# One encoder layer with attention and a recurrent branch: the elementwise work around the merge of its branches, written for VectorE in place of GpSimd

## The chip, the cores and the metric

The kernel runs on one core of a Trainium2 chip. The metric is the device time of one execution in microseconds. A core has five instruction queues that each run in program order: TensorE (PE, with its weight loads shown as PEld), VectorE (DVE), ScalarE (ACT), GpSimd (POOL) and SyncE (SP, which here issues DMAs). They wait for each other through semaphores.

## What is computed

Two request groups, 1024 and 256 tokens, share all weights and run as 1280 columns. Cut to what matters here:

```
h = rmsnorm(x, norm_mix) * (1 + sc1) + sh1;  p = h @ w_in
o_mla  = mla_branch(p_mla) @ w_mla_o
y      = wkv_scan(forward) + wkv_scan(backward)
mu, var = mean and variance of y over each head of 64
yn     = (y - mu) * rsqrt(var + LNX_EPS) * lnx_w + lnx_b
out    = (yn + bonus) * g;      o_rwkv = out @ w_rwkv_o
x = x + g1 * ((sigmoid(gate_m) * o_mla + sigmoid(gate_r) * o_rwkv) @ w_out)
h = rmsnorm(x, norm_ffn) * (1 + sc2) + sh2      (the second norm)
x = x + g2 * ((silu(u) * z) @ w_ffn_out);  u, z = split(h @ w_ffn_in)
return rmsnorm(x, final_norm)
```

## The kernel before, in words

Activations lie with channels on the 128 partitions (eight tiles of 128 channels) and tokens along the free axis. A product of f32 accuracy is made of three passes in the rounded format fp32r: each operand is split into a high part (a cast on ACT) and a low part (the f32 value minus the high part), and PE sums high x high, low x high and high x low. A weight tile comes by DMA into `wraw`, ACT makes `whi` (L53), and a subtraction makes `wlo` (L55). `split_w` takes the engine of that subtraction as an argument and uses POOL if none is given. Activations are split by `split_in` (L1023 on ACT, then L1024, on DVE if no engine is given).

The order of instructions on each engine is made by a scheduler from the program's order and priorities; each engine then runs its list in order. The stage around the change goes like this.

- While the recurrent scan ends (its last triangular inversion is the alternating pair L865 and L867 on DVE), PE fills in the gate products and the attention output product (`mla_out`, with its sums L1172 and the low parts of its weights on POOL). The first `branch` call, for the columns 256 to 768, runs beside it.
- `branch` loads the two scan outputs `y` and `yb`, adds them (L1064), subtracts the mean of each head (L1065 to L1067), squares on ACT (L1068), sums (L1069), makes the inverse deviation in a few small operations (L1071 to L1076), scales (L1078), transposes on PE (L1085), multiplies (L1086), adds the bonus (L1087) and splits the result (`or`, L1023 and L1024). It is called three times; the second and third calls, for the late columns, are spread through the first merge.
- `merge` runs first for the early columns (256 to 768) and then for the late ones (768 to 1280 and 0 to 256). For each of eight output tiles `dt` it has a product with `w_rwkv_o` (L1041, four weight tiles deep, one `split_w`), a multiplication by the gate (L1102), the addition of the attention part `xm` (L1103) and a split into `h2h` and `h2l` (L1023, L1024). Then, again for eight tiles, comes the product with `w_out` (two `split_w`) and the residual (L1115). `gt` and `xm` come by DMA into a pool of four row buffers, so that two `dt` are in flight in the early merge and one, of two pieces each, in the late merge. The split weights have two buffers.
- `norm2` squares and sums x1 (L1212 on ACT, L1213), multiplies by the inverse norm (L1217) and by the modulation (L1221), and splits (L1023, L1024), two tiles of three on POOL. It runs for the early columns inside the late merge, and for the late ones inside the first FFN product.
- The FFN after it (`gemm`, L67) is one unbroken row of matmuls.

The buffer counts of the row, product and weight pools stand in one line:

```
QB, MR, FR, KS, FP, RB, WB = 3, 4, 4, 4, 2, 2, 2
```

Of the kernel before, what the change touches and what calls it, by code (L numbers as in the profile page):

```python
# [18 lines left out]
KT = D // P  # L19
# [1006 lines left out]

def weights(g, src, kt):
    return [split_w(g, src[:, k0:k0 + 4, :], 4, pool=g.fl, tag=g.ft, rbufs=RB, bufs=WB) for k0 in range(0, kt, 4)]


def product(g, src, kt, parts, ws=None):

    ws = ws or weights(g, src, kt)
    for part in parts:
# [12 lines left out]
def branch(g, c0, n, tile_, row, out, ps):  # L1047
# [12 lines left out]
    for w in range(nw):  # L1060
        y, yb = tile_("y"), row("yb")
        for t, nm in ((y, "y0"), (yb, "y1")):
            nc.sync.dma_start(out=t, in_=g.scr[nm][c0 + w * P:c0 + (w + 1) * P, :])
        nc.gpsimd.tensor_tensor(y, y, yb, ALU.add)  # L1064
        nc.vector.tensor_reduce(mean[:, 8 * w:8 * w + 8], heads(y), AX.X, ALU.add)  # L1065
# [11 lines left out]
    for w, y in enumerate(ys):  # L1077
        (nc.gpsimd if w % 2 else nc.vector).tensor_tensor(heads(y), heads(y), each(rs, w), ALU.mult)  # L1078
    for j in range(4):
# [6 lines left out]
        nc.vector.tensor_tensor(wg, wg, p, ALU.mult)  # L1086
        nc.gpsimd.tensor_tensor(wg, wg, bg, ALU.add)  # L1087
        split_in(g, wg, out[0][:, j, :], out[1][:, j, :])


def merge(g, spans, ops, m, x1, row):
# [3 lines left out]
    for dt in range(KT):  # L1095
        ts = []
        for c, (c0, n) in zip(cs, spans):
            ts.append((row("gt")[:, :n], row("xm")[:, :n]))
            for t, nm, k in zip(ts[-1], ("gate", "xm"), (8, 0)):
                nc.sync.dma_start(out=t, in_=g.scr[nm][k + dt, :, c])  # L1100
        for p, c, (t, xm) in zip(product(g, io["w_rwkv_o"][dt], 4, [[x] for x in ops]), cs, ts):
            nc.vector.scalar_tensor_tensor(t, t, 1.0, p, ALU.add, ALU.mult)  # L1102
            nc.gpsimd.tensor_tensor(t, t, xm, ALU.add)  # L1103
            split_in(g, t, m[0][:, dt, c], m[1][:, dt, c])
    for dt in range(KT):
        xs = [row("xt")[:, :n] for _, n in spans]
        for c, x in zip(cs, xs):
            nc.sync.dma_start(out=x, in_=io["xT"][dt, :, c])
        for p, x, (c0, n) in zip(product(g, io["w_out"][dt], KT, [[([y[:, :, c] for y in m], n)] for c, (_, n) in zip(cs, spans)]),
                                 xs, spans):  # L1110
            for s, (s0, l) in enumerate(SEG):
# [85 lines left out]
def phase_ffn(g, out, mid):  # L1197
# [8 lines left out]
    def norm2(ms, c0, n):  # L1206
# [8 lines left out]
        for k in range(KT):  # L1215
            h = ms.tile([P, n], F32, tag="q", name="h", bufs=QB)
            nc.vector.tensor_tensor(h, x1[:, k, c], acc, ALU.mult)  # L1217
            for s, (s0, l) in enumerate(SEG):
                lo, hi = max(c0, s0) - c0, min(c0 + n, s0 + l) - c0
                if lo < hi:  # L1220
                    nc.vector.tensor_scalar(h[:, lo:hi], h[:, lo:hi], g.A2[:, k, s:s + 1], g.modT[:, 24 + k, s:s + 1],  # L1221
                                            ALU.mult, ALU.add)
            split_in(g, h, hh[:, k, c], hl[:, k, c], nc.vector if k % 3 == 1 else nc.gpsimd)

# [237 lines left out]
```

## Time and profile before

| | us |
|---|---|
| three runs, median (lowest to highest) | 2691.51 (2689.03 to 2695.47) |
| the profiled execution, its own time | 2687.72 |
| span of its trace | 2686.0 |
| PE busy in the span | 2501.3 (93%) |
| DVE busy | 1426.3 (53%) |
| ACT busy | 998.8 (37%) |
| POOL busy | 800.6 (30%) |
| mean granted clock of TensorE, share of full | 0.958 |

The busy figures are averages over stages with different limits. The stage that the change touches runs from about 1376 to 1780 us after the start of the span. "Idle before" in a row is the time for which the engine stood still just ahead of such an instruction; the name behind an arrow is what ended that time.

### The profile page before, as it was taken

To read this page: it belongs to the slowest core of one execution; us is meant where nothing else is said; L and a number is where in the kernel's file an instruction comes from. 1 tells how busy PE (TensorE), PEld (TensorE's weight loads), DVE (VectorE), ACT (ScalarE), POOL (GpSimd) and SP (SyncE) were. 2 spreads that over 40 slices of the span, in tenths; PEclk is the share of its full clock that TensorE was granted. 3 is DMA by queue.
4 is the path that set the end of the run, shared out by engine and by line. 5 is a ranking of instruction groups with operands and counts; after the bars stand their busy time and mean duration, and the time that the engine had idled before them with its cause. 6 is when DMAs were issued, how large, how long until landed. Compare 5 with 4: busy or idle time off the path is not lost.

```text
span 2686.0 us, 42442 instructions
## 1 busy us (share of the span) xinstructions
PE 2501.3 (93%) x17018; PEld 2121.5 (79%) x17018; DVE 1426.3 (53%) x2399; ACT 998.8 (37%) x1867; POOL 800.6 (30%) x789
## 2 busy tenths in 40 slices
PE   5999999989998799999898898899999999999997
PEld 3777777778887688888886677778888888888886
DVE  5655652357777688886785666552222232222328
ACT  4422332347676765555652233331110111101114
POOL 2112131021015655443434665442111111111123
PEclk7999999999999798899998999999999999999998
DMA  7654532100003545644656754221111111111113
GB/s 285 230 197 174 212 126 84 47 31 19 18 13 89 186 146 173 176 129 139 202 172 193 240 167 144 80 71 56 40 33 39 40 40 40 35 37 40 40 42 132
DMA packets 188470, 292.37 MB, mean 109 GB/s; under 512 B 16160, under 2 KB 106096, under 8 KB 188272
## 3 DMA queue, kind: packets, MB, share of 16 engines
q1 hardware_dynamic: 174880, 242.07, 28.4%
q0 software_dynamic: 5760, 26.22, 2.4%
q10 hardware_dynamic: 7632, 21.37, 2.3%
q8 instruction: 134, 2.20, 0.3%
q14 instruction: 64, 0.52, 0.1%
HBM read 211.95 MB, written 77.64 MB: 108 GB/s over the span
## 4 chain that ended last, share of the span: by engine, by line
PE 72%; DVE 16%; DMA 4%; issue 3%; POOL 2%; ACT 2%; SPq 0%; POOLq 0%; DVEq 0%; ACTq 0%
PE mm L67 43%; PE fp L1041 8%; PE s L627 3%; DVE xt L865 3%; DVE W L867 2%; PE o L661 2%; PE proj L560 2%; PE gps L453 2%; PE t L648 2%; PE pA L820 1%; PE py L913 1%; PE py L931 1%; PE ada_ps L170 1%; PE lora L369 1%; PE pS L925 1%
## 5 line engine op out<-in xcount | busy, mean ns | idle before, releaser
L55 POOL TENSOR_TENSOR wlo<-wraw,whi 128x1024 fp32r<-128x1024 f32 (+3 forms) x197 | 359.5, 1827 | 1168.0 <-ACT whi L53 1151.9
L53 ACT CAST whi<-wraw 128x1024 fp32r<-128x1024 f32 (+2 forms) x212 | 172.7, 818 | 917.3 <-issue 460.4
L67 PE MATMUL mm<-h2h,whi 128*128 128x512 f32 (+1 forms) x1056 | 279.5, 358 | 2.8 <-ACT whi L53 2.7
L67 PE MATMUL mm<-h2h,wlo 128*128 128x512 f32 (+1 forms) x1056 | 278.8, 358 | 2.7 <-POOL wlo L55 2.7
L67 PE MATMUL mm<-h2l,whi 128*128 128x512 f32 (+1 forms) x1056 | 278.3, 357 | 0.0
L67 PE MATMUL mm<-g,whi 128*128 128x512 f32 (+1 forms) x1056 | 240.7, 359 | 6.2 <-DVE ft L1251 5.6
L1041 PE MATMUL fp<-x,whi 128*128 128x256 f32 (+1 forms) x912 | 203.0, 316 | 15.0 <-ACT x L1023 8.3
L67 PEld LDWEIGHTS mm<-g,whi 128*128 128x128 f32 x1056 | 177.8, 190 | 38.0 <-issue 5.7
L67 PEld LDWEIGHTS mm<-h2h,whi 128*128 128x128 f32 x1056 | 177.2, 189 | 34.5 <-ACT whi L53 3.3
L67 PEld LDWEIGHTS mm<-h2h,wlo 128*128 128x128 f32 x1056 | 177.0, 189 | 34.3 <-POOL wlo L55 3.6
L67 PEld LDWEIGHTS mm<-h2l,whi 128*128 128x128 f32 x1056 | 177.1, 189 | 31.3 <-issue 0.5
L1263 DVE SCALAR_TENSOR_TENSOR x<-mm,g2h,x 128x512 f32<-128x512 f32 (+1 forms) x144 | 87.0, 656 | 196.3 <-PE mm L67 196.0
L1041 PEld LDWEIGHTS fp<-x,whi 128*128 128x128 f32 x912 | 153.5, 200 | 25.4 <-ACT x L1023 10.0
L1251 DVE SCALAR_TENSOR_TENSOR ft<-ft,mm 128x512 f32<-128x512 f32 (+1 forms) x66 | 36.0, 593 | 226.9 <-ACT ft L1250 226.9
L67 PE MATMUL mm<-hh,whi 128*128 128x512 f32 (+1 forms) x480 | 148.8, 368 | 6.9 <-ACT pp L320 3.9
L1041 PE MATMUL fp<-x,wlo 128*128 128x256 f32 (+1 forms) x456 | 144.4, 317 | 11.6 <-POOL wlo L55 7.6
L67 PE MATMUL mm<-hl,whi 128*128 128x512 f32 (+1 forms) x480 | 148.2, 365 | 7.0 <-DVE hl L265 6.9
L1252 DVE TENSOR_TENSOR ft<-ft,mm 128x512 f32<-128x512 f32 (+1 forms) x66 | 36.0, 593 | 217.5 <-PE mm L67 217.5
L67 PE MATMUL mm<-hh,wlo 128*128 128x512 f32 (+1 forms) x480 | 146.5, 365 | 0.0
L67 PE MATMUL mm<-g,wlo 128*128 128x512 f32 (+1 forms) x528 | 136.2, 359 | 1.2 <-POOL wlo L55 1.2
L865 DVE TENSOR_TENSOR xt<-W,X 128x126 f32<-128x126 f32 (+22 forms) x310 | 127.6, 412 | 9.0
L867 DVE TENSOR_TENSOR W<-W,xt 128x126 f32<-128x126 f32 (+22 forms) x310 | 125.0, 403 | 8.6
(320 smaller groups left out, 5210.7 us busy)
## 6 DMA issues: line engine op xcount, KB each, us to landing
wraw<-in_w_ffn_in_dram SPq DMA_DIRECT2D x56, 512.0 KB, 3.5
araw<-in_w_ada_dram ACTq DMA_DIRECT2D x32, 512.0 KB, 3.3
wraw<-in_w_ffn_out_dram SPq DMA_DIRECT2D x26, 512.0 KB, 3.6
wraw<-in_w_in_dram SPq DMA_DIRECT2D x20, 512.0 KB, 3.8
x<-scr_h SPq DMA_DIRECT2D x20, 512.0 KB, 7.7
whi<-scr_gw SPq DMA_DIRECT2D x36, 256.0 KB, 3.2
wlo<-scr_gw SPq DMA_DIRECT2D x36, 256.0 KB, 3.5
araw<-in_w_ada_dram SPq DMA_DIRECT2D x16, 512.0 KB, 9.4
```

Source lines behind the costliest of these rows:

```text
L53: nc.scalar.copy(hi, raw)
L55: (eng or nc.gpsimd).tensor_tensor(lo, raw, hi, ALU.subtract)
L67: nc.tensor.matmul(p[:, :n], lhsT=ww[:, k, :], rhs=aa[:, k, c0:c0 + n], start=(k == 0 and i == 0), stop=(k == kt - 1 and i == 2))
L453: nc.tensor.matmul(p[:, :n], lhsT=ww[:, k % 4, :], rhs=aa[:, k, c0:c0 + n], start=(k == 0 and i == 0), stop=(k == KT - 1 and i == 2))
L560: nc.tensor.matmul(p[:, :n], lhsT=ww[:, k, :], rhs=aa[:, k, c0:c0 + n], start=(k == 0 and i == 0), stop=(k == kt - 1 and i == 2))
L627: nc.tensor.matmul(s[:, o:o + w], lhsT=a[:, tt * P:(tt + 1) * P], rhs=b[:, c0 + o:c0 + o + w], start=(m == 0), stop=(m == 2))
L648: nc.tensor.transpose(t[:, j, :], prs[i][:, kk * P:(kk + 1) * P], g.ident)
L661: nc.tensor.matmul(o, lhsT=vs[h // 4][:, c0 // P + kk, h % 4, :], rhs=pts[j][m][kk // 4][:, kk % 4, :], start=(kk == 0 and m == 0), stop=( ...
L865: nc.vector.tensor_tensor(tv, W[:, h:, j:j + 1].broadcast_to([P, n, j]), X[:, j:j + 1, 0:j].broadcast_to([P, n, j]), ALU.mult)
L867: nc.vector.tensor_tensor(W[:, h:, 0:j], W[:, h:, 0:j], tv, ALU.add)
L1041: g.nc.tensor.matmul(p[:, c:c + n], lhsT=ww[:, k % 4, :], rhs=aa[:, k, :n], start=(k == 0 and i == 0), stop=(k == kt - 1 and i == 2))
L1263: nc.vector.scalar_tensor_tensor(x1[:, dt, c0:c0 + n], p[:, :n], g.g2h[:, dt, c0 // TP:c0 // TP + 1], x1[:, dt, c0:c0 + n], ALU.mult, ALU.add)
```

## The change

Every tensor operation that POOL had in `branch`, `merge` and `norm2` is written for DVE: the sums L1064, L1087 and L1103, the scaling L1078 (every second one was on POOL), the low parts of the weights of both merge products (L55, through a new argument of `weights` and `product`) and the low parts of the second norm (L1024, two of three were on POOL). POOL keeps the low parts of the other weights and L1172.

```diff
-def weights(g, src, kt):
-    return [split_w(g, src[:, k0:k0 + 4, :], 4, pool=g.fl, tag=g.ft, rbufs=RB, bufs=WB) for k0 in range(0, kt, 4)]
+def weights(g, src, kt, eng=None):
+    return [split_w(g, src[:, k0:k0 + 4, :], 4, eng, pool=g.fl, tag=g.ft, rbufs=RB, bufs=WB) for k0 in range(0, kt, 4)]
...
-def product(g, src, kt, parts, ws=None):
+def product(g, src, kt, parts, ws=None, eng=None):
...
-    ws = ws or weights(g, src, kt)
+    ws = ws or weights(g, src, kt, eng)
...
-        nc.gpsimd.tensor_tensor(y, y, yb, ALU.add)
+        nc.vector.tensor_tensor(y, y, yb, ALU.add)
...
-        (nc.gpsimd if w % 2 else nc.vector).tensor_tensor(heads(y), heads(y), each(rs, w), ALU.mult)
+        nc.vector.tensor_tensor(heads(y), heads(y), each(rs, w), ALU.mult)
...
-        nc.gpsimd.tensor_tensor(wg, wg, bg, ALU.add)
+        nc.vector.tensor_tensor(wg, wg, bg, ALU.add)
...
-        for p, c, (t, xm) in zip(product(g, io["w_rwkv_o"][dt], 4, [[x] for x in ops]), cs, ts):
+        for p, c, (t, xm) in zip(product(g, io["w_rwkv_o"][dt], 4, [[x] for x in ops], eng=nc.vector), cs, ts):
...
-            nc.gpsimd.tensor_tensor(t, t, xm, ALU.add)
+            nc.vector.tensor_tensor(t, t, xm, ALU.add)
...
-        for p, x, (c0, n) in zip(product(g, io["w_out"][dt], KT, [[([y[:, :, c] for y in m], n)] for c, (_, n) in zip(cs, spans)]),
-                                 xs, spans):
+        for p, x, (c0, n) in zip(product(g, io["w_out"][dt], KT, [[([y[:, :, c] for y in m], n)] for c, (_, n) in zip(cs, spans)],
+                                         eng=nc.vector), xs, spans):
...
-            split_in(g, h, hh[:, k, c], hl[:, k, c], nc.vector if k % 3 == 1 else nc.gpsimd)
+            split_in(g, h, hh[:, k, c], hl[:, k, c], nc.vector)
```

The scheduler makes new lists from it. DVE in the early merge, among the products with `w_rwkv_o`, before (names as above; `gn` holds the small statistics of `branch`):

```order
L1024 TENSOR_TENSOR h2l<-gt,h2h 128x512
L1102 SCALAR_TENSOR_TENSOR gt<-gt,fp 128x512 x2
L1086 TENSOR_TENSOR wg<-wg,yT 128x512 x2
L1024 TENSOR_TENSOR h2l<-gt,h2h 128x512
L1102 SCALAR_TENSOR_TENSOR gt<-gt,fp 128x512
L1024 TENSOR_TENSOR h2l<-gt,h2h 128x512
L1024 TENSOR_TENSOR or<-wg,or 128x512
L1102 SCALAR_TENSOR_TENSOR gt<-gt,fp 128x512
```

and with the change, at the same place:

```order
L55 TENSOR_TENSOR wlo<-wraw,whi 128x512
L1103 TENSOR_TENSOR gt<-gt,xm 128x512
L1102 SCALAR_TENSOR_TENSOR gt<-gt,fp 128x512
L1067 TENSOR_TENSOR y<-y,gn 128x512
L55 TENSOR_TENSOR wlo<-wraw,whi 128x512
L1103 TENSOR_TENSOR gt<-gt,xm 128x512
L1024 TENSOR_TENSOR h2l<-gt,h2h 128x512
L1069 TENSOR_REDUCE gn<-yb 128x8
L1102 SCALAR_TENSOR_TENSOR gt<-gt,fp 128x512
L55 TENSOR_TENSOR wlo<-wraw,whi 128x512
L1024 TENSOR_TENSOR h2l<-gt,h2h 128x512
```

The whole loop of an output tile (L1102, L1103, L1024) now lies on DVE, with the low part of a weight tile (L55) in every turn.

DVE in the late merge, where the products with `w_rwkv_o` end and those with `w_out` begin, before (`x_15708` is x1; `acc` and `q` belong to the second norm):

```order
L1024 TENSOR_TENSOR h2l<-gt,h2h 128x512
L1024 TENSOR_TENSOR h2l<-gt,h2h 128x256
L1115 SCALAR_TENSOR_TENSOR x_15708<-fp,gh,xt 128x256 x6
L1213 TENSOR_TENSOR acc<-acc,q 128x512
L1115 SCALAR_TENSOR_TENSOR x_15708<-fp,gh,xt 128x256 x3
L1213 TENSOR_TENSOR acc<-acc,q 128x512
```

and with the change:

```order
L1115 SCALAR_TENSOR_TENSOR x_15708<-fp,gh,xt 128x256 x6
L55 TENSOR_TENSOR wlo<-wraw,whi 128x512
L1213 TENSOR_TENSOR acc<-acc,q 128x512
L55 TENSOR_TENSOR wlo<-wraw,whi 128x512 x2
L1115 SCALAR_TENSOR_TENSOR x_15708<-fp,gh,xt 128x256 x3
L1213 TENSOR_TENSOR acc<-acc,q 128x512
L55 TENSOR_TENSOR wlo<-wraw,whi 128x512 x2
```

Two low parts of weights now stand between one tile's residual (L1115) and the next one's, behind L1213, which waits for ACT's square.

## Rows read from the trace of the kernel before

**Rows 1.** Stretches of the stage: PE, PEld, DVE, ACT, POOL busy us (instructions), PEclk, DMA share, GB/s.

```profile
1376.00:1440.00 64.00, 49.56 (x411) 39.45 (x409) 58.93 (x113) 19.82 (x34) 32.77 (x25) 0.90 0.68 216
...
1503.00:1555.00 52.00, 40.64 (x157) 28.85 (x157) 43.99 (x54) 17.61 (x32) 43.76 (x30) 0.93 0.75 241
1555.00:1600.00 45.00, 42.84 (x190) 33.34 (x190) 23.43 (x36) 16.49 (x30) 25.49 (x21) 1.00 0.49 150
1600.00:1650.00 50.00, 41.80 (x219) 34.75 (x220) 42.26 (x56) 16.23 (x32) 36.19 (x28) 0.96 0.49 150
1650.00:1710.00 60.00, 60.00 (x335) 51.97 (x334) 15.33 (x32) 12.96 (x22) 18.68 (x15) 0.98 0.35 107
1710.00:1750.00 40.00, 28.76 (x112) 21.46 (x110) 32.86 (x52) 18.04 (x29) 24.20 (x11) 0.90 0.30 91
```

**Rows 2.** Waits of PE from 1370 to 1790 us: total us, times, longest.

```profile
PE fp L1041 <- POOL wlo L55: 11.7, 13, 1.7
...
PE nb_ps L83 <- DVE acc L1213: 5.8, 2, 4.6
```

**Rows 3.** Line L1078 alone: ns minimum/median/maximum, first and last start.

```profile
L1078 DVE TENSOR_TENSOR y<-y,gn x5: 674/691/1527, 1410.7 to 1561.5; 128x512 f32<-128x512 f32 x5
L1078 POOL TENSOR_TENSOR y<-y,gn x5: 1087/1484/2374, 1410.7 to 1561.6; 128x512 f32<-128x512 f32 x5
```

**Rows 4.** DVE's group L1102 from 1370 to 1790 us (busy us, mean ns | idle before).

```profile
L1102 DVE SCALAR_TENSOR_TENSOR gt<-gt,fp 128x512 f32<-128x512 f32 x16 | 10.7, 680 | 3.2 <-DMA gt<-scr_gate 2.4 <-PE fp L1041 0.6
```

**Rows 5.** DVE in order of time (start us, us), two instructions back to back.

```profile
1393.03 0.69 DVE L1067 TENSOR_TENSOR y<-y,gn 128x512 f32<-128x512 f32 x1
1393.63 0.68 DVE L1065 TENSOR_REDUCE gn<-y 128x8 f32<-128x512 f32 x1
```

**Rows 6.** DVE's inversion pair from 1310 to 1374 us, before the first branch.

```profile
L867 DVE TENSOR_TENSOR W<-W,xt 128x110 f32<-128x110 f32 (+22 forms) x41 | 14.1, 345 | 1.3
L865 DVE TENSOR_TENSOR xt<-W,X 128x110 f32<-128x110 f32 (+22 forms) x41 | 12.3, 300 | 1.3
```

**Rows 7.** The same pair from 1376 to 1440 us, beside the first branch.

```profile
L865 DVE TENSOR_TENSOR xt<-W,X 128x126 f32<-128x126 f32 (+22 forms) x31 | 17.1, 550 | 0.6
L867 DVE TENSOR_TENSOR W<-W,xt 128x126 f32<-128x126 f32 (+22 forms) x31 | 15.7, 505 | 0.5
```

**Rows 8.** DVE's groups in the early merge, 1503 to 1555 us.

```profile
L1024 DVE TENSOR_TENSOR h2l<-gt,h2h 128x512 fp32r<-128x512 f32 x8 | 10.6, 1322 | 3.3 <-ACT h2h L1023 3.3
L1024 DVE TENSOR_TENSOR or<-wg,or 128x512 fp32r<-128x512 f32 x8 | 8.2, 1035 | 0.0
...
L1067 DVE TENSOR_TENSOR y<-y,gn 128x512 f32<-128x512 f32 x4 | 4.8, 1210 | 0.0
```

**Rows 9.** DVE's groups in the late merge, 1600 to 1650 us.

```profile
L1217 DVE TENSOR_TENSOR h<-x,acc 128x512 f32<-128x512 f32 x8 | 11.2, 1414 | 0.0
L1024 DVE TENSOR_TENSOR h2l<-gt,h2h 128x512 fp32r<-128x512 f32 x7 | 8.1, 1150 | 3.8 <-ACT h2h L1023 3.8
```

**Rows 10.** DVE in order of time in the late products with `w_out`.

```profile
1675.59 0.88 DVE L1115 SCALAR_TENSOR_TENSOR x<-fp,gh,xt 128x256 f32<-128x256 f32 x2 [6.16 <-PE fp L1041]
...
1677.16 0.69 DVE L1213 TENSOR_TENSOR acc<-acc,q 128x512 f32<-128x512 f32 x1
1684.01 0.88 DVE L1115 SCALAR_TENSOR_TENSOR x<-fp,gh,xt 128x256 f32<-128x256 f32 x2 [6.16 <-PE fp L1041]
```

**Rows 11.** POOL in order of time there.

```profile
1677.71 1.29 POOL L55 TENSOR_TENSOR wlo<-wraw,whi 128x512 fp32r<-128x512 f32 x1 [3.26 <-ACT whi L53]
1681.60 1.28 POOL L55 TENSOR_TENSOR wlo<-wraw,whi 128x512 fp32r<-128x512 f32 x1 [2.59 <-ACT whi L53]
```

**Rows 12.** DVE's largest group in the second norm, 1710 to 1750 us.

```profile
L1221 DVE TENSOR_SCALAR h<-h,A,modT 128x256 f32<-128x256 f32 x16 | 12.0, 805 | 0.0
```

**Rows 13.** POOL's groups there.

```profile
L55 POOL TENSOR_TENSOR wlo<-wraw,whi 128x1024 fp32r<-128x1024 f32 x6 | 14.8, 2474 | 12.9 <-ACT whi L53 12.9
L1024 POOL TENSOR_TENSOR h2l<-h,h2h 128x512 fp32r<-128x512 f32 x5 | 9.5, 1904 | 8.2 <-ACT h2h L1023 8.2
```

## The prediction, made before the changed kernel had run

> **What bounds the kernel now.** Read first the busy times by stretch [rows 1]: PE is what the program waits for nearly everywhere, and where PE never stands still, as from 1650 to 1710 us, no change of another engine can gain anything. So the reader looks for stretches in which PE has idle time and in which DVE and POOL are both near full. There are four: the end of the scan (1376 to 1440, PE idle 64.0 - 49.6 = 14.4 us, DVE busy 58.9), the early merge (1503 to 1555, idle 11.4, DVE 44.0 and POOL 43.8 of 52), the late merge (1600 to 1650, idle 8.2, DVE 42.3, POOL 36.2) and the second norm (1710 to 1750, idle 11.2, DVE 32.9 of 40). Their idle time is 45 us in all, and the granted clock is below full in each (0.90 to 0.96), which costs PE some more. That is the pool a gain can come from. The waits of PE [rows 2] say who ends its idle time: POOL's low parts of weights for 11.7 us in 13 waits, DVE's norm sums for 5.8; the rest is spread over DVE's and ACT's splits.
>
> Next, how long one operation takes. L1078 is the same operation on both engines at the same time [rows 3]: POOL 1.48 us median, DVE 0.69, but on DVE up to 1.53. L1102, of the same width but with one operand in PSUM, never shows that: its mean is 0.680 over 16 [rows 4]. So a DVE operation with both inputs in SBUF is held up while POOL works, and one with an input in PSUM is not. The size of it by stretch: the inversion pair takes 0.300 and 0.345 us where POOL has little to do [rows 6] and 0.550 and 0.505 beside the first branch [rows 7]; the splits of the early merge take 1.32 and 1.04 instead of 0.69 [rows 8], and the norm's products in the late merge 1.41 [rows 9]. Two DVE instructions back to back start 0.60 us apart [rows 5], so 0.60 is what one more in a full row costs, and about 0.35 at half the columns (an estimate, half the width and the same ends).
>
> **The change, part by part.** 114 instructions leave POOL: 48 low parts of weights (2 merges of 8 tiles with 1 + 2 weight tiles), 10 of L1064, 5 of L1078, 12 of L1087, 24 of L1103, 15 of L1024; 17 of them have half the columns. On DVE they add 97 x 0.60 + 17 x 0.35 = 64 us to a stage of 400. The question in each stretch is whether the hold-up that goes is as large as the work that comes, and whether PE waited for it.
>
> *End of the scan.* Ten of POOL's 25 instructions there move (4 L1064, 2 L1078, 4 L1087): + 10 x 0.60 = 6.0 us on DVE. The pair is held up by 31 x 0.250 + 31 x 0.160 = 12.7 us [rows 6, 7]; POOL keeps 15 of its 25, so 10/25 of that, 5.1, goes. DVE's work stays as it is, 58.9 + 0.9. POOL's weights for the attention product no longer queue behind L1078 and L1087. I take 0, with - 5 (all of the 5.1 gained, the new work in DVE's 5.1 us of idle time) and + 4 (the new work ahead of the scan's steps, two thirds of 6.0).
>
> *Early merge.* Here POOL has nothing left. + 30 x 0.60 = 18.0 us for DVE, and at least 8 x 0.63 + 8 x 0.345 + 4 x 0.52 = 9.9 us of hold-up go [rows 8]: 44.0 + 8.1 = 52 of 52, less what the new list carries over into the next stretch, where DVE has 21.6 us free. DVE stays the engine with least room, then; but the loop of one tile gets shorter. With two tiles in flight on four row buffers, a turn is: load, L1102, L1103, cast, L1024, next load. L1103 falls from POOL's 1.48 [rows 3] to 0.69 and L1024 from 1.32 to 0.69, 1.4 us less per turn and 8/2 x 1.4 = 5.7 us over the stretch; the first split of `or`, which PE waits for, comes some 2 us sooner (0.79 on each of L1078 and L1087, 0.35 on the split). Against that stands the low part of a weight, 0.60, in every turn. I take - 5, ends - 9 (both links and PE's low clock) and + 2.
>
> *Early product with w_out.* PE-bound: 42.8 of 45. Every half tile, 45 / 16 = 2.8 us, PE needs a fresh low part; POOL took 1.3 us for it, DVE takes 0.69 but only when its row of instructions reaches it, behind L1115 (which waits for PE) and the third branch call. + 1, ends - 2 and + 4.
>
> *Late merge.* 28 instructions, 21 full and 7 half: + 12.6 + 2.5 = 15.1 us on DVE, and 8 x 0.72 + 7 x 0.46 = 9.0 at least go [rows 9]: 42.3 + 6.1 = 48 of 50. One tile is in flight, so each link counts 8 times: L1103 - 0.79 and L1024 - 0.46 are 8 x 1.25 = 10.0 us, of which PE's idle 8.2 is the most that can be had, and a DVE this full gives back the greater part. I take - 3, ends - 8 and + 5.
>
> *Late product with w_out.* No gain is possible (PE 60.0 of 60). Is there a loss? After a tile's residual, L1213 ends at 1677.16 + 0.69 = 1677.85; POOL's low part ran from 1677.71 to 1679.00 [rows 10, 11], DVE's would run from 1677.85 to 1678.5, sooner. The next one starts on POOL at 1681.60, and DVE is free until 1684.01. 0, at most + 2 for the third tile, whose low part the new list puts behind six residuals.
>
> *Second norm.* Five splits of 1.90 us leave POOL [rows 13], + 5 x 0.60 = 3.0 on DVE. L1221 takes 0.805 at 256 columns [rows 12]; POOL's remaining low parts for the FFN, 14.8 of its 24.2 us, go on holding DVE up. If 0.40 is its own time (an estimate: below L1078's 0.69 by the width), 16 x 0.40 = 6.5 are hold-up and 40% of it, 2.6, goes. DVE is even; the FFN's low parts no longer queue behind splits on POOL, one split of 1.9 us each. - 2, ends - 4 and + 1.
>
> The sum is 0 - 5 + 1 - 3 + 0 - 2 = - 9 us. Against the profiled execution, 2687.7, that is 2678.7; the median of the runs stands 3.8 us higher, at 2691.5, and so the forecast for a median is 2682.
>
> The Trainium skill, Perfetto Trace Analysis, section Optimizing Scalar/DVE Operations, speaks against the direction of this change: with a saturated DVE, it says, giving some work to ScalarE or even GpSimd can pay, and it adds that the two share an SBUF read port, so that moving work between them may not help. By the first half DVE would pay for every added instruction; by the second the hold-up goes with it, as [rows 3, 4] let one expect.
>
> **The rivals.** *DVE is merely filled again.* The hold-up that goes is as large as the work that comes, in every full stretch (58.9 to 59.8, 44.0 to 52, 42.3 to 48), and the shorter loops are eaten by queueing. PE's idle time stays. 0 to - 5: 2687 to 2691. For it: the arithmetic above. Against it: POOL's 43.8 and 36.2 us were a second full queue in the same chain, and that queue is gone.
>
> *Slower: PE waits for low parts that stand behind a waiting DVE instruction.* Place: the early product with w_out. DVE runs L1115, which PE releases, then L1213, which ACT's square releases, then branch work that waits for DMAs, and only then L55, while PE needs one every 2.8 us. Price: 1 us per half tile is 16 us, 2691 + 16 - 5 for the earlier early merge = 2702. It decides from the point at which more than 2.8 - 0.69 = 2.1 us, that is three instructions or one DMA wait, come between the cast and its low part. For it: DVE's idle ahead of L1102 is already ended by a DMA [rows 4]. Against: the steady rhythm of [rows 10].
>
> *Slower by the first half of the Trainium skill's rule:* the long DVE times have another cause than POOL, and the work comes with no relief. Then the early merge pays 18.0 less its 8.0 idle, the late 15.1 less 7.7, the scan 6.0 less 5.1: 2691.5 + 10 + 7.4 + 0.9 = 2710. The difference between L1078 and L1102 speaks against it [rows 3, 4].
>
> *The change does less than it says:* at the end of the scan and in the second norm POOL keeps 15 of 25 and 6 of 11 instructions, so that the hold-up stays there; this is in the terms above.
>
> **How the numbers follow.** About 0.2%, 5.4 us, is what a measurement of this kernel can tell from no change. The forecast, faster by some 6 to 25 us (2666 to 2686), has 0.58; DVE merely filled again 0.24; the wait behind DVE 0.14; the rule's case 0.04. So faster 0.58, within 0.2% 0.24, slower 0.18. The likeliest time is 2682. The range runs from 2667, where the early and late merges give most of their idle time (- 9, - 8, - 4, - 4 for the other two), to 2694, which takes in the second case and the beginning of the third.
>
> **What would show it.** In the changed profile the splits of the early merge should take 0.69 us instead of 1.32, L1217 in the late merge 0.69 instead of 1.41, the inversion pair about 0.45. POOL should be empty between the attention product and the first FFN weights. PE's waits for low parts should fall from 11.7 us to under 6, and the early merge should be some 5 us shorter. I am wrong if PE's waits for L55, now on DVE, are longer than before; if the hold-up stays; or if the time between the first L1102 and the last h2l of a merge does not fall.

## The result, and the profile after

| | before | changed |
|---|---|---|
| median of five runs each, us (lowest to highest) | 2691.51 (2689.03 to 2695.47) | 2670.30 (2666.16 to 2674.54) |
| ratio, 95% interval | | 0.9929 (0.9912 to 0.9946) |
| span of the profiled execution, us | 2686.0 | 2672.8 |
| DVE busy, POOL busy in the span, us | 1426.3, 800.6 | 1439.4, 645.9 |

The kernel became faster by 19.1 us by the ratio (0.0071 x 2691.5; the two medians lie 21.2 apart) where 9.5 were forecast. In a later series of runs the same kernel gave 0.9961 (0.9948 to 0.9975), 10.5 us. The two intervals do not overlap, so an interval does not cover what changes from one series to the next, and ratios of different series are compared below only with the traces beside them. The stage itself, read in one trace from each of the two series, became 14 to 17 us shorter. POOL lost 155 us of work, and DVE's busy time grew by only 13, though 64 us of work (the prediction's estimate) came to it.

The ends of the two spans do not compare directly. The code ahead of the stage is the same in both kernels, and it ran 3.6 us later in the trace of after (in the traces of the experiments 0.1 to 10.1 later, and never earlier). So stretches are measured between the starts of the same instructions. The cuts are: the start of the last L865 of the last inversion but one (1363.14 us before), the end of the last L871, PE's first product on `or`, the 8th, 9th and 24th L1102, PE's first FFN matmul (`h2h`), its first matmul of the second FFN product (`g`), and the end of DVE's last instruction. Two of the borders are only roughly the ends of PE's products: in the changed kernel 14 of the early merge's matmuls come behind the 8th L1102 instead of ahead of it, and 16 to 18 of the late merge's come ahead of the 24th instead of behind it. So the two stretches of a merge are best read together: - 6.9 and - 6.2 for the early merge, - 7.6 and - 6.2 for the late one.

| stretch, us | before | change | the same kernel again |
|---|---|---|---|
| end of the scan, with the first branch call | 77.2 | + 5.2 | + 6.6 |
| rest of the attention product | 63.4 | + 1.3 | + 0.3 |
| early merge, first product | 41.8 | - 7.2 | - 7.0 |
| early product with `w_out` | 51.9 | + 0.3 | + 0.8 |
| late merge, first product | 53.0 | - 5.4 | - 5.3 |
| late product with `w_out` | 64.9 | - 2.2 | - 0.9 |
| first FFN product, with the late second norm | 126.6 | - 8.9 | - 8.9 |
| from there to the end | 840.4 | + 0.1 | + 0.4 |
| sum | 1319.3 | - 16.8 | - 14.0 |

The stretches repeat to within 1.5 us, and nothing is given back later. Now the views. Busy times, columns as in [rows 1], of four stretches between these cuts (end of the scan, first product of the early merge, of the late merge, first FFN product), before:

```profile
1363.14:1440.32 77.18, 62.15 (x668) 51.28 (x665) 63.47 (x121) 27.36 (x47) 34.39 (x26) 0.92 0.67 211
1503.70:1545.53 41.83, 33.87 (x132) 24.47 (x132) 35.72 (x46) 14.25 (x26) 34.95 (x25) 0.92 0.75 244
1597.43:1650.44 53.01, 44.80 (x238) 37.45 (x237) 43.37 (x58) 17.33 (x33) 38.44 (x29) 0.96 0.48 148
1715.36:1841.99 126.63, 119.20 (x585) 99.40 (x585) 66.02 (x93) 42.03 (x69) 55.03 (x27) 0.95 0.23 71
```

and with the change:

```profile
1366.79:1449.15 82.36, 63.74 (x675) 52.30 (x673) 64.67 (x133) 28.83 (x49) 24.21 (x19) 0.88 0.68 212
1513.86:1548.45 34.59, 30.96 (x118) 22.49 (x119) 31.30 (x60) 13.27 (x24) 0.00 (x0) 0.95 0.78 254
1600.66:1648.30 47.64, 44.73 (x254) 38.15 (x252) 42.20 (x88) 17.73 (x33) 0.00 (x0) 1.00 0.56 171
1711.04:1828.73 117.69, 116.19 (x585) 97.23 (x585) 61.27 (x103) 42.45 (x69) 42.26 (x17) 0.98 0.25 77
```

In the early merge DVE runs 60 instructions where it ran 46, and is busy for less time, 31.3 us against 35.7. PE's idle time (length less PE busy) falls from 8.0 to 3.6 us, from 8.2 to 2.9 and from 7.4 to 1.5. PE's waits from 1370 to 1790 us [rows 2]:

```profile
PE fp L1041 <- ACT x L1023: 18.4, 8, 10.1
PE fp L1041 <- DVE wlo L55: 3.3, 6, 1.5
...
PE py L913 <- DVE tt L885: 2.2, 1, 2.2
...
PE nb_ps L83 <- DVE acc L1213: 1.2, 1, 1.2
```

The wait for low parts fell from 11.7 to 3.3 us, that for the norm's sums from 5.8 to 1.2. New are 2.2 us for the copy L885 at the end of the scan and 10 us more for the inputs of the attention product. DVE's groups from 1503 to 1555 us, for the most part the early merge [rows 8]:

```profile
L55 DVE TENSOR_TENSOR wlo<-wraw,whi 128x512 fp32r<-128x512 f32 x12 | 8.1, 685 | 0.5 <-ACT whi L53 0.5
L1103 DVE TENSOR_TENSOR gt<-gt,xm 128x512 f32<-128x512 f32 x8 | 5.5, 686 | 1.6 <-DMA xm<-scr_xm 1.6
...
L1024 DVE TENSOR_TENSOR h2l<-gt,h2h 128x512 fp32r<-128x512 f32 x8 | 5.4, 675 | 0.0
...
L1067 DVE TENSOR_TENSOR y<-y,gn 128x512 f32<-128x512 f32 x4 | 2.7, 685 | 0.0
```

The split `h2l` takes 0.675 us instead of 1.322. In the late merge [rows 9], and then in the late second norm [rows 12]:

```profile
L1024 DVE TENSOR_TENSOR h2l<-gt,h2h 128x512 fp32r<-128x512 f32 x8 | 5.5, 683 | 0.0
...
L1217 DVE TENSOR_TENSOR h<-x,acc 128x512 f32<-128x512 f32 x8 | 5.2, 682 | 0.0
```

```profile
L1217 DVE TENSOR_TENSOR h<-x,acc 128x512 f32<-128x512 f32 x8 | 7.9, 1003 | 3.7 <-ACT acc L103 3.7
L1221 DVE TENSOR_SCALAR h<-h,A,modT 128x256 f32<-128x256 f32 x16 | 7.7, 533 | 0.0
...
L1213 DVE TENSOR_TENSOR acc<-acc,q 128x256 f32<-128x256 f32 x7 | 4.1, 592 | 0.4
```

Where POOL is empty, as in both merges, every DVE operation has its own time, that is, the one it takes with nothing beside it. In the late norm POOL still makes FFN low parts, and L1217 is still at 1.00.

The end of the scan shows the loss. DVE in order of time, before:

```profile
1375.79 2.03 DVE L856 STREAM_TRANSPOSE X<-aa 128x1024 f32<-128x1024 f32 x1 [3.35 <-PE pw L882]
1377.85 0.69 DVE L885 COPY tt<-pw 32x512 f32<-32x512 f32 x1
```

and with the change:

```profile
1379.58 2.03 DVE L856 STREAM_TRANSPOSE X<-aa 128x1024 f32<-128x1024 f32 x1 [3.48 <-PE pw L882]
1381.58 1.76 DVE L1064 TENSOR_TENSOR y<-y,yb 128x512 f32<-128x512 f32 x1
1383.36 0.69 DVE L885 COPY tt<-pw 32x512 f32<-32x512 f32 x1
...
1427.77 0.68 DVE L1181 SCALAR_TENSOR_TENSOR gt<-gt,fp 128x512 f32<-128x512 f32 x1
1431.87 0.69 DVE L1087 TENSOR_TENSOR wg<-wg,bg 128x512 f32<-128x512 f32 x1 [3.42 <-DMA bg<-scr_bg]
```

L1064 now stands between the transposition and the copy that PE's scan step waits for, and is itself held up (1.76 us; POOL makes a low part from 1381.52 to 1382.78); and later DVE stands still for 3.42 us at L1087, in the middle of the inversion, until `bg` has come. POOL had waited at such a sum before too, for 1.72 us, and the inversion had not stood behind it.

The late norm shows the largest gain. DVE before, and POOL beside it:

```profile
1745.80 4.13 DVE L1213 TENSOR_TENSOR acc<-acc,q 128x256 f32<-128x256 f32 x2
```

```profile
1740.04 2.94 POOL L1024 TENSOR_TENSOR h2l<-h,h2h 128x512 fp32r<-128x512 f32 x1 [0.88 <-ACT h2h L1023]
1744.80 4.84 POOL L55 TENSOR_TENSOR wlo<-wraw,whi 128x1024 fp32r<-128x1024 f32 x2 [1.83 <-ACT whi L53]
```

The last two sums of the norm, of 0.41 us each where they run freely, took 4.13 beside POOL's low parts, and PE waited 4.6 us for them. While PE stood still its granted clock fell, to a mean of 0.66 of full from 1746 to 1756 us (part of that time at the lower of its two levels, 1.2 GHz, the rest at 2.4 GHz); with the change each ten us from 1716 to 1806 is at the upper level. Columns as in [rows 1], before and after:

```profile
1746.00:1756.00 10.00, 5.93 (x17) 4.89 (x18) 6.52 (x12) 2.81 (x4) 3.64 (x2) 0.66 0.37 105
```

```profile
1746.00:1756.00 10.00, 10.00 (x45) 8.03 (x44) 5.11 (x10) 2.92 (x5) 4.22 (x2) 1.00 0.29 79
```

That adds up to the gain of this stretch: the same 585 matmuls run in both kernels, PE stands still for 5.9 us less (7.4 to 1.5), and its busy time falls by 3.0 (119.2 to 116.2) at the higher mean clock (0.95 to 0.98).

### The profile page after: what moved, and what is told of

It is laid out like the page before. It is cut to its first block, busy times and chain, and to the rows that moved or that the text cites. A ratio compares the mean times of both kernels' runs of the same rounds, so it can differ in the third digit from the quotient of the medians.

```text
span 2672.8 us, 42383 instructions
## 1 busy us (share of the span) xinstructions
PE 2498.4 (93%) x17018; PEld 2121.9 (79%) x17018; DVE 1439.4 (54%) x2513; ACT 999.9 (37%) x1867; POOL 645.9 (24%) x675
## 5 line engine op out<-in xcount | busy, mean ns | idle before, releaser
L55 POOL TENSOR_TENSOR wlo<-wraw,whi 128x1024 fp32r<-128x1024 f32 (+2 forms) x149 | 293.9, 1975 | 1343.3 <-ACT whi L53 1129.8
L1041 PE MATMUL fp<-x,whi 128*128 128x256 f32 (+1 forms) x912 | 206.9, 320 | 27.5 <-ACT x L1023 18.4
L865 DVE TENSOR_TENSOR xt<-W,X 128x126 f32<-128x126 f32 (+22 forms) x310 | 125.8, 406 | 9.0
## 6 DMA issues: line engine op xcount, KB each, us to landing
araw<-in_w_ada_dram SPq DMA_DIRECT2D x16, 512.0 KB, 10.1
```

Of the source, the lines that this page charges most:

```text
L55: (eng or nc.gpsimd).tensor_tensor(lo, raw, hi, ALU.subtract)
L865: nc.vector.tensor_tensor(tv, W[:, h:, j:j + 1].broadcast_to([P, n, j]), X[:, j:j + 1, 0:j].broadcast_to([P, n, j]), ALU.mult)
L1041: g.nc.tensor.matmul(p[:, c:c + n], lhsT=ww[:, k % 4, :], rhs=aa[:, k, :n], start=(k == 0 and i == 0), stop=(k == kt - 1 and i == 2))
```

## The experiments

The theory (S, with H for its mechanism) is that each part of the change earns in its own stretch, by the hold-up of DVE and the waits for POOL that go with it, and that the first branch call loses. Change of each stretch against the trace of before, in us, with the cuts of the table above ("merges" takes four of them together), and the timed ratio:

| run | what is on DVE, beyond before | scan end | attention | merges | late norm | sum | ratio (95%) |
|---|---|---|---|---|---|---|---|
| | the whole change | + 5.2 | + 1.3 | - 14.5 | - 8.9 | - 16.8 | 0.9929 (0.9912 to 0.9946) |
| x11_again | the whole change | + 6.6 | + 0.3 | - 12.5 | - 8.9 | - 14.0 | 0.9961 (0.9948 to 0.9975) |
| x1_norm | second norm | + 1.4 | + 0.6 | - 2.0 | - 6.8 | - 6.2 | 0.9973 (0.9961 to 0.9985) |
| x8_wlo | low parts of merge weights | - 2.5 | + 0.3 | - 5.8 | - 1.5 | - 9.4 | 0.9958 (0.9945 to 0.9971) |
| x2_merge | the same and L1103 | + 0.1 | + 1.9 | - 11.6 | + 0.3 | - 9.4 | 0.9964 (0.9950 to 0.9978) |
| x3_branch | all three branch calls | + 4.7 | + 1.4 | - 2.0 | - 1.5 | + 2.7 | 1.0009 (0.9995 to 1.0023) |
| x10_two | low parts of merge weights and norm | - 1.9 | - 0.4 | - 10.0 | - 8.8 | - 20.9 | 0.9942 (0.9921 to 0.9962) |
| x4_bgpool | all but L1087 of the first call | + 5.2 | + 2.0 | - 12.8 | - 9.0 | - 14.4 | 0.9949 (0.9937 to 0.9962) |
| x6_l1064 | all but L1064 of the first call | + 2.3 | - 0.8 | - 15.6 | - 8.9 | - 22.9 | 0.9922 (0.9909 to 0.9936) |
| x5_first | all but the first call | - 2.0 | + 2.2 | - 15.2 | - 8.8 | - 23.7 | 0.9907 (0.9893 to 0.9920) |
| x9_ffn | as x5_first, and 8 FFN low parts | - 2.9 | + 2.5 | - 15.0 | - 10.4 | - 25.8 | 0.9921 (0.9904 to 0.9938) |
| x7_dummy | whole, and idle work on POOL | + 6.9 | + 1.7 | - 10.6 | - 0.6 | - 2.4 | 0.9998 (0.9985 to 1.0012) |
| x12_hold | as x9_ffn, and idle work on POOL | - 2.0 | + 2.3 | - 13.2 | - 9.3 | - 22.1 | 0.9930 (0.9906 to 0.9954) |

The sums are taken from single traces; the timed differences lie within some 5 us of them. The runs x1 to x4 were timed in one series, x5 to x8 in one, x9 to x11 in one, and x12 by itself. Where the first branch call is left as it was, the end of the scan varies from - 2.9 to + 1.4, so that 2 us there say nothing.

**The parts alone.** Second norm, from the kernel before:

```diff
-            split_in(g, h, hh[:, k, c], hl[:, k, c], nc.vector if k % 3 == 1 else nc.gpsimd)
+            split_in(g, h, hh[:, k, c], hl[:, k, c], nc.vector)
```

> Kernel before, with the low parts of the second norm (L1024, 15 of 24) on DVE and nothing else changed. Theory S (each stretch keeps its own gain): the stretch from the first to the second FFN product, 126.6 us in the kernel before and 117.7 with the whole change, falls here too, to about 118; PE's 4.6 us wait for the last L1213 goes; the time is 8 to 9 us under that of before, ratio 0.997. Rival C (POOL's remaining work holds DVE up wherever it is, so that a part of the change gives far less than its share): ratio 0.9985 or more. Rival N (the gain of this stretch was an accident of one trace): no difference, ratio 1.000.

Measured - 7.3 us (0.9973), and - 6.8 in the stretch of the late norm: theory S. PE's wait for the last L1213 is still 2.0 us here, not gone.

The merges, all else as before (with `weights` and `product` as in the change):

```diff
-        for p, c, (t, xm) in zip(product(g, io["w_rwkv_o"][dt], 4, [[x] for x in ops]), cs, ts):
+        for p, c, (t, xm) in zip(product(g, io["w_rwkv_o"][dt], 4, [[x] for x in ops], eng=nc.vector), cs, ts):
...
-            nc.gpsimd.tensor_tensor(t, t, xm, ALU.add)
+            nc.vector.tensor_tensor(t, t, xm, ALU.add)
...
+                                         eng=nc.vector), xs, spans):
```

> Kernel before, with the low parts of both merge weights (L55) and the sum L1103 on DVE; branch and second norm as before. Theory S: the early merge gains 5 us, the late one 3 (its second norm still on POOL), the products with w_out 0 to 2; ratio 0.996 to 0.997, and DVE's h2l splits of the early merge below 0.9 us. Rival C: the branch work left on POOL keeps the splits at 1.1 us or more, and the ratio is 0.999 to 1.000.

Measured - 9.7 us (0.9964), theory S by the time; its splits show the dose: 0.858 us, between the 1.322 of before and the 0.675 of the whole change. The gains did not fall where they were expected: the products with `w_out`, expected at 0 to 2 us, gained 5.4, and the first products 6.2 (3.9 early, 2.3 late).

The branch, all else as before:

```diff
-        nc.gpsimd.tensor_tensor(y, y, yb, ALU.add)
+        nc.vector.tensor_tensor(y, y, yb, ALU.add)
...
-        (nc.gpsimd if w % 2 else nc.vector).tensor_tensor(heads(y), heads(y), each(rs, w), ALU.mult)
+        nc.vector.tensor_tensor(heads(y), heads(y), each(rs, w), ALU.mult)
...
-        nc.gpsimd.tensor_tensor(wg, wg, bg, ALU.add)
+        nc.vector.tensor_tensor(wg, wg, bg, ALU.add)
```

> Kernel before, with L1064, L1078 and L1087 of all three branch calls on DVE, and nothing else. Theory S: the first call loses about 5 us, because a sum L1087 that waits for its DMA now stands ahead of the inversion on DVE; the later two calls give 0 to 2 us back; ratio 1.001 to 1.002, slower. Rival: the 5 us of the trace come from elsewhere (the start of the attention product, a clock step), and the first call is even; ratio 0.999 to 1.000.

Measured + 2.4 us (1.0009); the interval takes in 1, so the time does not tell theory S from the rival. The trace does: the end of the scan lost 4.7 and PE waited 2.2 us for L885, as with the whole change. So this loss belongs to the branch on DVE.

The low parts of the merge weights without L1103; against x2_merge:

```diff
-            nc.vector.tensor_tensor(t, t, xm, ALU.add)
+            nc.gpsimd.tensor_tensor(t, t, xm, ALU.add)
```

> Kernel before, with only the low parts of the weights of both merge products (48 L55) on DVE; L1103 and everything else as before. With both, the gain was 10.8 us (ratio 0.9964). If the low parts carry it (PE waited 11.7 us for them): 0.9965 to 0.998, and PE's waits for L55 below 5 us. If the loop of a tile carries it (L1103 on POOL 1.48 us, now 0.69, and POOL's reads beside the splits): 0.999 or more.

Its time lies on the side of the first case (0.9958, a little beyond the range of 0.9965 to 0.998), but its trace does not fit it: PE's waits for low parts did not fall below 5 us. In the two products of each merge it gains 5.8 us where x2_merge gains 11.6; the rest of its 9.4 is the chance at the end of the scan (- 2.5) and in the late norm. DVE's groups from 1503 to 1560 us, and PE's waits from 1500 to 1715:

```profile
L55 DVE TENSOR_TENSOR wlo<-wraw,whi 128x512 fp32r<-128x512 f32 x13 | 12.3, 953 | 1.1 <-ACT whi L53 1.1
L1024 DVE TENSOR_TENSOR h2l<-gt,h2h 128x512 fp32r<-128x512 f32 x8 | 9.2, 1154 | 0.1
```

```profile
PE fp L1041 <- DVE wlo L55: 14.6, 10, 3.8
```

PE waits longer for low parts than before (14.6 us here, 11.7 in the longer stretch of [rows 2]): they stand in DVE's row behind splits that are held up (1.154), and are held up there themselves (0.953), as POOL still works. With L1103 moved as well, the same wait is 4.7. The low parts alone and L1103 after them earn about 6 us each, and the four parts add up: - 5.8 (low parts) - 5.8 (L1103, 11.6 less 5.8) - 2.0 (norm) - 2.0 (branch) = - 15.6, against - 14.5 and - 12.5 with all of them.

x10_two is x8_wlo with the edit of x1_norm:

> Kernel before, with two parts of the change alone: the low parts of the merge weights and those of the second norm on DVE; branch and L1103 as before. Theory S (gains add up, and the other parts bring nothing): - 10.9 (x8_wlo alone gave 10.4 to 11.3) - 7.3 (x1_norm) = - 18, ratio 0.993, as the whole change (0.9929), and no loss at the end of the scan. Rival: L1103 or the later branch calls on POOL hold the merges up once the low parts are gone; - 12 to - 15, ratio 0.9945 to 0.9955. Third possibility: with no first branch call on DVE it comes out as x5_first, ratio 0.9907.

In its trace theory S holds: - 10.0 in the merges and no loss at the end of the scan, so that the sum, - 20.9, is below the whole change's. Timed in the series of x11_again it was 0.9942, at the edge of the rival's range, with the whole change beside it at 0.9961; the two intervals overlap. The rival is right in part: L1103 and the later branch calls are worth 5 us more (x5_first, - 15.2 in the merges).

**The loss at the end of the scan.** `branch` gets an engine for its first call; in x4_bgpool L1087 alone uses it, in x6_l1064 L1064 alone, in x5_first both and every second L1078:

```diff
-def branch(g, c0, n, tile_, row, out, ps):
+def branch(g, c0, n, tile_, row, out, ps, eng=None):
...
-        nc.vector.tensor_tensor(wg, wg, bg, ALU.add)
+        (eng or nc.vector).tensor_tensor(wg, wg, bg, ALU.add)
...
-               lambda name: pa.tile([P, 512], F32, tag="pa", name=name))
+               lambda name: pa.tile([P, 512], F32, tag="pa", name=name), g.nc.gpsimd)
```

> Whole change, but the four sums L1087 of the first branch call stay on POOL. If the wait of DVE for the DMA of bg (3.4 us between two steps of the inversion) is what the end of the scan lost, the inversion ends 3 to 5 us sooner and the time is 3 to 5 us below that of the whole change (2670), ratio to before 0.991 to 0.992. Rival: the row of the scheduler, not this wait, sets the end of the inversion, or PE waits elsewhere for the time won; 2670 again, ratio 0.993.

A miss: 0.9949 was measured where 0.991 to 0.992 was expected, and the end of the scan lost the same 5.2 us as with the whole change. The inversion did end 3.1 us sooner (+ 1.7 at its last L865 against + 4.8), but the new list put a split of the attention input ahead of the inversion's last transposition:

```profile
1446.36 1.04 DVE L869 STREAM_TRANSPOSE dt<-W 128x512 f32<-128x512 f32 x1
1449.61 1.50 DVE L1024 TENSOR_TENSOR x<-raw,x 128x512 fp32r<-128x512 f32 x1 [2.21 <-ACT x L1023]
1451.03 0.70 DVE L871 STREAM_TRANSPOSE xr<-dt 128x512 f32<-128x512 f32 x1
```

DVE waits 2.21 us there, through ACT and POOL's L1172, for a transfer, the split then takes 1.50 us instead of 0.69, and the gain is gone: one wait of this kind was exchanged for another.

> Whole change, but the first branch call (beside the end of the scan) keeps all its POOL work: L1064, every second L1078, L1087. Theory L (the first sum L1064, which on DVE stands between the transposition L856 and the copy L885 that PE waits for, with three more L1064 behind it, is what the end of the scan lost): the stretch from the inversion's 278th step to the end of L871 loses 5.2 us less, and the time is 2665 to 2667, ratio 0.991. Rival D (the loads of raw and bc for the attention product set the time there, since PE waits 10 us for them whatever the inversion does): the inversion ends sooner, PE's wait grows, 2670 again, ratio 0.993.

> Whole change, but only the four sums L1064 of the first branch call stay on POOL. Theory L: the 4 us lost by the 285th step of the inversion come back, while DVE's wait for bg at L1087 (3.4 us in the trace of the whole change) stays; ratio 0.991 to 0.992. Rival D: 0.993 as with the whole change, PE waiting for the attention inputs instead.

Theory L: with L1064 alone on POOL the stretch loses 2.3 us instead of 5.2 to 6.6, with the whole call on POOL nothing (- 2.0). In x5_first L885 follows L856 at once, and DVE waits for POOL's sum only behind it:

```profile
1379.47 2.03 DVE L856 STREAM_TRANSPOSE X<-aa 128x1024 f32<-128x1024 f32 x1 [3.40 <-PE pw L882]
1381.53 0.69 DVE L885 COPY tt<-pw 32x512 f32<-32x512 f32 x1
1382.25 0.19 DVE L865 TENSOR_TENSOR xt<-W,X 128x31 f32<-128x31 f32 x1
1383.74 0.69 DVE L1065 TENSOR_REDUCE gn<-y 128x8 f32<-128x512 f32 x1 [1.30 <-POOL y L1064]
```

PE's wait for the attention inputs was not the limit (rival D): it is 7.8 us in x5_first and 18.4 with the whole change, from 1370 to 1500 us. x5_first and the whole change were not timed in one series, and its interval overlaps that of the first timing; the traces give it 7 to 10 us.

**The gain of the late norm: hold-up of DVE, or the row on POOL?** Idle POOL work at the places where POOL had the splits; nobody reads its result, and the lists of the other engines stay as they are:

```diff
             split_in(g, h, hh[:, k, c], hl[:, k, c], nc.vector)
+            if k % 3 != 1:
+                for s0 in range(0, n, 192):
+                    l = min(192, n - s0)
+                    v = hh[:, k, c0 + s0:c0 + s0 + l].bitcast(F32)
+                    nc.gpsimd.tensor_tensor(ms.tile([P, 192], F32, tag="junk", name="junk")[:, :l], v, v, ALU.subtract)
```

> Whole change, plus idle work on POOL in the second norm: for each tile whose low part POOL had before, POOL subtracts the tile h2h from itself in pieces of 192 columns into a scratch tile that nobody reads. The lists of DVE, PE and ACT are those of the whole change. Theory H (POOL's reads of SBUF lengthen DVE's operations, and that, not the link through POOL's own split, made the second norm slow): L1221, L1217 and L1213 of the late norm go up again to 0.75 us and more, and the stretch from the first to the second FFN product goes back from 117.7 us to 122 to 126; ratio 0.995 to 0.996. Rival Q (the split on POOL was a slow link between the norm's three buffers): nobody waits for the idle work, the stretch stays at 118 to 119 and the ratio at 0.993.

The stretch went back to 126.0 us, all but 0.6 of what had been won, and the late merge's first product lost 3.7 of its 5.4. So the loss needs no link Q, since nobody waits for this work; that the link had no share of its own in the kernel before is not shown. But DVE was held up and PE waited for POOL's FFN low parts too; DVE's groups from 1705 to 1760 us and PE's waits from 1695 to 1800:

```profile
L1024 DVE TENSOR_TENSOR h2l<-h,h2h 128x512 fp32r<-128x512 f32 x8 | 8.0, 1030 | 0.0
...
L1213 DVE TENSOR_TENSOR acc<-acc,q 128x256 f32<-128x256 f32 x7 | 6.9, 986 | 0.4
```

```profile
PE mm L67 <- POOL wlo L55: 5.7, 3, 3.6
```

So the loss has the size of the one before, but another wait makes it: PE waits 5.7 us for FFN low parts that come late (2.7 before, 1.5 with the change) and no longer for the last sum L1213 of this stretch (4.6 before). To part the two, the FFN's first low parts went to DVE, on the kernel of x5_first, without the idle work and then with it:

```diff
-            pu = gemm(g, split_w(g, io["w_ffn_in"][f0 + j], KT), (hh, hl), KT, chunks)
-            pz = gemm(g, split_w(g, io["w_ffn_in"][NFF + f0 + j], KT, both and nc.vector), (hh, hl), KT, chunks)
+            pu = gemm(g, split_w(g, io["w_ffn_in"][f0 + j], KT, chunks is early and nc.vector), (hh, hl), KT, chunks)
+            pz = gemm(g, split_w(g, io["w_ffn_in"][NFF + f0 + j], KT, (both or chunks is early) and nc.vector), (hh, hl), KT, chunks)
```

> Whole change with the first branch call on POOL as in the kernel before (the run x5_first), and in addition the low parts of the eight weight tiles of the first FFN group, which run beside the late second norm, on DVE: POOL is then empty there. The stretch from the first to the second FFN product was 117.7 to 117.8 us with all lists that have the second norm on DVE. Theory H (what is left of POOL's reads still lengthens DVE there: L1217 1.0, L1254 1.1 to 1.6 us): L1217 falls to 0.69, L1254 to 0.7, PE's waits for low parts go, the stretch falls to 114 to 116; ratio 0.989 to 0.990. Rival F (DVE is full in this stretch, and 8 x 1.1 us more on it come ahead of the norm): L1217 falls, but PE waits for L55 on DVE or for the norm's splits; 118 to 121, ratio 0.991 to 0.992.

> The kernel of x9_ffn (POOL empty beside the late second norm) plus the idle POOL work of x7_dummy: POOL subtracts each tile h2h, for which it had the low part before, from itself into a scratch tile. Nobody waits for POOL in the stretch now: the low parts of the first FFN group are on DVE, and the lists of DVE, PE and ACT are those of x9_ffn. In x7_dummy the stretch between the FFN products lost 8.3 us, but there FFN low parts stood behind the idle work on POOL. Theory H (it is the hold-up of DVE by POOL's reads): L1221, L1213 and L1024, 0.41, 0.42 and 0.69 us in x9_ffn, rise to 0.55, 0.9 and 1.0, and the stretch, 116.2 us in x9_ffn, is 119 to 124; ratio 0.994 to 0.996. Rival P (it was the row on POOL: FFN low parts behind the splits): DVE's operations may lengthen, but PE does not wait, and the stretch is 116 to 117; ratio 0.992.

DVE's groups from 1700 to 1750 us in x9_ffn, POOL empty:

```profile
L55 DVE TENSOR_TENSOR wlo<-wraw,whi 128x1024 fp32r<-128x1024 f32 x8 | 9.7, 1224 | 2.8 <-ACT whi L53 2.8
L1221 DVE TENSOR_SCALAR h<-h,A,modT 128x256 f32<-128x256 f32 x16 | 5.7, 408 | 0.0
L1217 DVE TENSOR_TENSOR h<-x,acc 128x512 f32<-128x512 f32 x8 | 5.3, 686 | 1.2 <-ACT acc L103 1.2
...
L1213 DVE TENSOR_TENSOR acc<-acc,q 128x256 f32<-128x256 f32 x7 | 3.0, 423 | 0.2
```

and from 1695 to 1750 in x12_hold:

```profile
L1221 DVE TENSOR_SCALAR h<-h,A,modT 128x256 f32<-128x256 f32 x16 | 6.7, 471 | 0.0
L1024 DVE TENSOR_TENSOR h2l<-h,h2h 128x512 fp32r<-128x512 f32 x8 | 6.2, 796 | 0.0
L1217 DVE TENSOR_TENSOR h<-x,acc 128x512 f32<-128x512 f32 x8 | 6.0, 772 | 1.2 <-ACT acc L103 1.2
L1213 DVE TENSOR_TENSOR acc<-acc,q 128x256 f32<-128x256 f32 x7 | 2.9, 417 | 0.2
```

Eight more low parts on DVE (9.7 us) made the stretch 1.5 us shorter, since the other groups shrank to their own times. That is theory H in direction, with 116.3 us just above its range of 114 to 116; the time, 0.9921, is not the 0.989 to 0.990 that H asked for. The idle work beside it cost 1.1 us (116.3 to 117.4, just above rival P's range), and no PE wait came back: PE stood still for 0.2 us in either. So rival P has the larger part in the loss of x7_dummy: this idle work is cheap by itself, and dear where FFN low parts stand behind it and come late. In x12_hold the sums L1213 were not held (0.417), in x7_dummy they were (0.986), by two FFN low parts of 2.5 us. The idle work is a weaker load than the splits that it stands for: its 15 pieces of at most 192 columns took 0.4 to 1.4 us each, the splits of 512 columns 1.3 to 2.9. What those splits would cost without FFN low parts on POOL was not tried.

**The best version.** x9_ffn, with 0.9921 beside 0.9961 for the whole change in one series, has intervals that do not overlap, and the shortest stage of all traces. x5_first, timed in another series at 0.9907, cannot be told from it by times.

x11_again has no edit against the changed kernel:

> The whole change again, beside the two others on one chip. All theories: ratio 0.992 to 0.994. Its trace says how far the stretches of one list vary between two executions: the loss at the end of the scan (5.2 us from the inversion's 278th step to the end of L871) and the gain between the FFN products (8.9 us) should both come back within 1 us if they belong to the list; if one of them was chance, it will not.

The end of the scan came back as + 6.6 (1.4 from the first, where 1 had been allowed), the late norm as - 8.9: both belong to the list, the first with a wider spread. The time, 0.9961, is outside what was expected; in its profiled execution the code ahead of the stage ran 5.3 us later than in the first trace, so part of the difference may lie where the two kernels are the same.

## Why the prediction was right in direction and short in size

- **The forecast**, faster by 9.5 us at 2682, was right in sign, and the 2670.3 us lie in the range. The signs it had named came: `h2l` 0.675 and L1217 0.682 us, the inversion pair 0.37 and 0.35 (about 0.45 had been named), POOL empty between the attention product and the FFN weights, PE's waits for low parts 3.3 us. The terms did not come out as priced: the end of the scan lost 5 to 7 us where nothing was forecast, and the merges together (- 14.5 and - 12.5 where - 7 was forecast) and the late norm gained 5.5 to 7.5 and 6.9 us more than their terms. That the later timing of 10.5 us is so near the forecast is luck: errors of opposite sign.
- **Early merge**, - 5: measured - 7.2 and - 7.0, inside its ends. The hold-up went as said (`h2l` 1.322 to 0.675 us), but DVE, forecast as full (52 of 52 us), was busy for 31.3 of 34.6, 4.4 us less than before. The step that failed is the balance 44.0 + 8.1: 30 instructions were counted into this stretch, and a net of 14 came to it (36 to the next); and every one in it runs in its own time, L1078 too (1.526 before), which had not been counted.
- **Early product**, + 1: + 0.3 and + 0.8. The wait behind a waiting DVE instruction that was feared there did not come; in x8_wlo, where PE waited 14.6 us for low parts, it waited for them for the most part in the first products, and not here. In x2_merge, x3_branch, x8_wlo and x10_two this stretch gained 3.4 to 5.2 us; why it did not with the whole change is not shown, and part of it is the border between the two stretches.
- **Late merge**, - 3: - 5.4 and - 5.3. "A DVE this full gives back the greater part" was wrong: it was busy for 42.2 of 47.6 us, not 48 of 50, and PE got 5.3 of its 8.2 idle us back.
- **Late product**, 0: - 2.2 and - 0.9, about the noise of a stretch.
- **Second norm**, - 2 with ends of - 4 and + 1: - 8.9 both times. The mis-sized term is the hold-up, 40% of 6.5 us. The own time of L1221 was estimated well (0.40; x9_ffn has 0.408), but L1213 was left out, which fell from 0.997 us to 0.592 each in the first trace, and with it the 4.6 us that PE waited for it, though [rows 2] have that wait. The clock behind the wait (a mean of 0.66 of full from 1746 to 1756 us) was not priced either. In the prediction's terms: it priced DVE's hold-up as a share of busy time, where PE's wait and the clock make up the gain (5.9 and 3.0 us).
- **End of the scan**, 0 with ends of - 5 and + 4: + 5.2 and + 6.6. The step that failed weighed added work against hold-up that goes, as if DVE were only full. That balance came out nearly as forecast (DVE 63.5 to 64.7 us between the cuts, + 1.2 for + 0.9), with the pair at 0.370 and 0.351 over its 31 steps, so that 10.4 us of hold-up went and not 5.1. But what counted was where the new instructions stand: L1064 in a chain that PE waits for, L1087 with a DMA to wait for inside the inversion. The prediction had new work ahead of the scan's steps only as its outer end of + 4; a wait behind a DVE instruction that waits for a DMA is the slower rival's mechanism, foreseen for another place.
- **The Trainium skill's advice** to take work off a saturated DVE (Perfetto Trace Analysis, Optimizing Scalar/DVE Operations) did not decide: with more work on DVE the merges became 12 to 15 us shorter. Its second half has the two engines share a read port; the trace agrees in that the hold-up went with the work (`h2l` 1.322 to 0.675 us), and no run here shows that it is a port.

## What to carry to other kernels

Work on POOL that reads SBUF was paid on DVE as well here, so that DVE could get more instructions and less busy time. Before moving an operation to DVE, look at what it waits for and what stands behind it in DVE's row: a sum that waits for a transfer belongs on the engine that nobody waits for. Price a stretch by the wait that PE has there, with its clock afterwards, and not by the balance of busy times alone.

## What had not been expected of the hardware

An operation with one tensor input in SBUF is held up by POOL too. L1221, a multiplication and addition with two scalars per partition, takes 0.408 us at 256 columns with POOL empty (x9_ffn), and 0.533 on the mean beside low parts of weights, 0.805 in the kernel before [rows 12]. The means hide what happens. Before and with the change, from 1710 to 1750 us (ns minimum/median/maximum):

```profile
L1221 DVE TENSOR_SCALAR h<-h,A,modT x16: 397/403/2485, 1721.7 to 1739.6; 128x256 f32<-128x256 f32 x16
```

```profile
L1221 DVE TENSOR_SCALAR h<-h,A,modT x16: 399/402/2490, 1717.4 to 1733.8; 128x256 f32<-128x256 f32 x16
```

Most are not slowed at all; with the change fifteen take 0.40 and one takes 2.49. The prediction had put the line between one and two inputs in SBUF, on the strength of L1102, whose other input is in PSUM, although its term for the second norm did count L1221 as held up. The Trainium skill, SBUF — State Buffer, section Who interferes with whom, counts `tensor_scalar` among the operations that can take the shared ports in a fast mode; the trace agrees that it is held. Its pace fits such a mode, which no run shows by itself: 256 columns more cost L1221 0.13 us (0.536 at 512 columns, POOL empty) and the sum L1213 0.27 (0.42 and 0.69).

A held operation waits for about the rest of POOL's instruction, so that it costs what that instruction is long and not a share. The two sums of 0.41 us that took 4.13 ended 0.3 us behind POOL's two low parts of 1024 columns (2.4 and 2.5 us each). Beside the idle pieces of x12_hold, of 192 columns at most, no L1221 of 256 columns took more than 0.67 us. Before leaving work on POOL beside a DVE chain, look at how long its single instructions are.
